# More gate tiles through DRAM, buffers from the room, weight splits on VectorE

## The chip, the cores and the metric

The kernel runs on one core of one Trainium2 chip. The metric is device time in microseconds from start to end of one execution; the median of three runs of the kernel before is 2383.82 us (2383.24 to 2390.1). TensorE is called PE, VectorE DVE, ScalarE ACT, GpSimd POOL and SyncE SP in the profile; PEld is TensorE's weight load.

## The reference, cut to what matters

Two blocks run on 512 tokens of width 1024 in float32. The first is a convolution and attention mixer, the second two attention variants followed by a feed-forward over retrieved experts. Only that last part is touched:

```python
def peer_ffn(x, w_q, sub_keys, expert_u, expert_v):       # 512 tokens, 1024 wide
    q = _rms((xt @ w_q).reshape(T, P_HEADS, P_KEY_DIM))    # 8 heads of 2 x 128
    s1 = einsum('thd,hnd->thn', q[..., :half], sub_keys[:, 0])   # 128 keys each
    s2 = einsum('thd,hnd->thn', q[..., half:], sub_keys[:, 1])
    v1, i1 = top_k(s1, 16); v2, i2 = top_k(s2, 16)
    vals, ci = top_k(all sums v1 + v2, 16)
    e = 128 * i1[ci // 16] + i2[ci % 16]                   # of 16384 experts
    g = softmax(vals)
    a = einsum('cd,ckd->ck', xc, expert_u[e])              # 128 experts a token
    w = g * gelu(a)
    return einsum('ck,ckd->cd', w, expert_v[e])
```

## The kernel before, in words

Matrix products keep nearly float32 precision by splitting each operand into a high half (rounded to float32r) and a low half (the rest): `split_into` copies the high half on ACT and subtracts the low half on DVE or POOL, and `mm3` makes three matmuls of each product. `chunk` loads a weight tile of 128x1024 on SP's queue into `wraw` (three buffers) and splits it into `whi` and `wlo` (two buffers each).

All stages up to about 1010 us (`block1`, `block2`) are not touched. `peer` then has three stages.

The **query stage**: for each of 16 half heads `n`, the queries are projected from `w3[n]` (512 tokens by 128), scored against 128 keys, and the best 16 found by searches on DVE (`top16`); after each second half `pairs` and `decode` combine the two. The projection of `n = 0` uses split weights. For the other fifteen, POOL first adds the halves of the input back into the tile `whole` (line 1382), and the weights are multiplied as they are, in full float32 (line 1397).

The **gate stage** (`gates`) turns the chosen experts and gates of the first 384 tokens into a dense matrix `wd` in DRAM, by one-hot matmuls (lines 1457 to 1470).

The **expert loop** (line 1533) runs over 128 blocks `e` of 128 experts for those 384 tokens. `up_tile(e)` multiplies a block of expert_u with the tokens (24 matmuls of 384 columns) and applies the Gelu. Line 1544 multiplies that tile with its gates, the product is split, and 18 matmuls of 512 columns (lines 84 to 86 under line 1554) add it, times the block of expert_v, to six accumulators `y`.

48 up tiles are made ahead, in the query and gate stages, while TensorE has other work too. 27 of these (`AHEAD`) stay in SBUF in tiles `gt`; 21 (`AWAY`, the last blocks) go to DRAM (`ud`, stored on SP's queue, line 1373) and come back in `gl`, three buffers, near the end of the loop (line 1559). The loop makes the other 80 itself, one in each of the first 80 blocks. So both the loop's weight tiles, for up and down, pass through the same three `wraw` and two `whi` and `wlo`; the up tile's low half is subtracted on POOL, the down tile's on DVE.

The last 128 tokens are not computed densely. `gathered` fetches, for each of the 128 chosen experts of a token, its row of expert_u and then of expert_v by an indirect DMA that POOL issues (line 1493) into one of four buffers `r4`. DVE reduces each row of expert_u with the tokens (line 1498) and adds each row of expert_v, weighted (line 1508). The 256 rows are spread over the loop by `work.advance`, 2.75 to a block in the first 80 blocks. `issue_after(self.pool_last)` keeps a gather behind the last subtract on POOL.

A scheduler sets each engine's order from the program; each engine then runs its own list in order and waits for semaphores.

Of the kernel before, what the change touches and what calls it, by code (L numbers as in the profile page):

```python
# [12 lines left out]
F32 = mybir.dt.float32  # L13
F32R = mybir.dt.float32r
# [4 lines left out]
ALU = mybir.AluOpType  # L19
# [25 lines left out]
class Builder:  # L45
    def __init__(self, tc, ins, out):
        self.tc = tc
        self.nc = tc.nc
        self.i = ins
        self.out = out  # L50


    def split(self, pool, src, tag, shape=None, bufs=None, hi_engine="act", lo_engine="dve"):
# [34 lines left out]
    def chunk(self, src, n=1024, lo_engine="dve"):  # L88

        nc = self.nc  # L90
        raw = self.wp.tile([128, 1024], F32, tag="wraw", name="wraw", bufs=3)
        hi = self.wp.tile([128, 1024], F32R, tag="whi", name="whi", bufs=2)
        lo = self.wp.tile([128, 1024], F32R, tag="wlo", name="wlo", bufs=2)
        nc.sync.dma_start(raw[:, :n], src)
        self.split_into(raw[:, :n], hi[:, :n], lo[:, :n], lo_engine=lo_engine)
        return hi, lo

    def stack_queries(self, src, q, scale=1.0):

# [1146 lines left out]
    def peer(self, hd, xn, xd):  # L1246


        nc, tc, bp = self.nc, self.tc, self.bp
        NT = 384  # L1250
        AHEAD = 27
        AWAY = 21
        NREST = 4
        with ExitStack() as s5:
            wk = s5.enter_context(tc.tile_pool(name="work5", bufs=1))
            ps = self.ps
            ps.share(mm="c", y2="d", y0="b", y1="b", y3="b", y4="a", y5="a")
            T = lambda tag, bufs=1, dt=F32, shape=(128, 512): wk.tile(list(shape), dt, tag=tag, name=tag, bufs=bufs)
# [3 lines left out]
            ud = self.dram.tile([AWAY, 128, NT], F32, name="ud")  # L1262
# [100 lines left out]
            def up_tile(e, lo_engine="pool"):  # L1363
                c = self.chunk(self.i["pu"][e], lo_engine=lo_engine)
                p = P()
                for k in range(8):
                    s = slice(k * 128, (k + 1) * 128)
                    self.mm3(p[:, :NT], (c[0][:, s], c[1][:, s]), (xn[0][k][:, :NT], xn[1][k][:, :NT]), k == 0, k == 7)
                away = e >= 128 - AWAY
                g = T("gs", 2, shape=(128, NT)) if away else T("gt", AHEAD, shape=(128, NT))  # L1370
                nc.scalar.activation(g, p[:, :NT], AF.Gelu_apprx_tanh)
                if away:
                    nc.sync.dma_start(ud[e - 128 + AWAY], g)
                else:
                    up[e] = g

            first_tiles = iter([*range(128 - AWAY, 128), *range(AHEAD)])


            whole = T("big", 2, shape=(128, 8, 512))  # L1380
            for k in range(8):
                nc.gpsimd.tensor_tensor(whole[:, k], xn[0][k], xn[1][k], op=ALU.add)

            for n in range(16):
                hd8, half = n // 2, n % 2
                with self.in_order(self.after if n < 2 else []):
                    if n % 4 == 0:
                        keys = T("r4", 4, shape=(128, 2, 512))[:, 0]
                        nc.sync.dma_start(keys, self.i["keys"][n // 4])
                    acc = P()  # L1390
                    if n == 0:
                        self.project(acc, self.chunk(w3[n], lo_engine="pool"), xn)
                    else:
                        w = self.wp.tile([128, 1024], F32, tag="wraw", name="wraw", bufs=3)
                        nc.sync.dma_start(w, w3[n])
                        for k in range(8):
                            nc.tensor.matmul(acc, w[:, k * 128:(k + 1) * 128], whole[:, k], start=k == 0, stop=k == 7)  # L1397
                q = T("r4", 4, shape=(128, 2, 512))[:, 0]
                nc.scalar.copy(q, acc)
                before, sq = sq, TP()  # L1400
                nc.scalar.activation(sq, acc, AF.Square)
                sp = P(f"y{(0, 1, 3, 4, 5)[n % 5]}")
                ks = slice(n % 4 * 128, n % 4 * 128 + 128)
                for b in range(4):
                    bs = slice(b * 128, b * 128 + 128)
                    nc.tensor.matmul(sp[:, bs], q[:, bs], keys[:, ks], start=True, stop=True)
                for b in range(4):
                    top16(val[:, b, hd8, half], idx[:, b, hd8, half], sp[:, b * 128:(b + 1) * 128], 128)
                if half == 1:
                    nc.gpsimd.tensor_tensor(sq, sq, before, op=ALU.add)  # L1410
                    for b in range(4):
                        nc.tensor.matmul(sv[:, b, hd8], sq[:, b * 128:(b + 1) * 128], self.ones[:, 0:2], start=True, stop=True)
                    pairs(hd8)
                    decode(hd8)
                for _ in range((0, 0, 0, 0, 2, 1)[min(n, 4 + n % 2)]):
                    up_tile(next(first_tiles))
# [20 lines left out]
            def gates():  # L1437


                for b in range(NT // 128):  # L1440
                    pt = P("y2")
                    for n, t in enumerate(chosen(b)):
                        nc.tensor.transpose(pt[:, n * 128:(n + 1) * 128], t, self.ident)
                    bs = slice(b * 128, (b + 1) * 128)
                    for n in (0, 2):
                        nc.scalar.copy(iT[n][:, bs], pt[:, n * 128:(n + 1) * 128])
                    second = wk.tile([128, 128, 8], BF16, tag="oh2", name="second", bufs=4)
                    nc.scalar.copy(second, pt[:, 128:256, None].to_broadcast([128, 128, 8]))
                    for tg in range(4):
                        wt = T("big", 2, shape=(128, 128, 32))  # L1450
                        for t4 in range(8):
                            hot = T("r4", 4, shape=(128, 2, 4, 128))
                            t0 = 128 * b + 32 * tg + 4 * t4
                            if t4 % 2 == 0:
                                short = wk.tile([128, 8, 128], BF16, tag="p", name="short", bufs=6)
                                of = second[:, t0 - 128 * b:t0 - 128 * b + 8]
                                nc.vector.tensor_tensor(short.rearrange("p t (a c) -> p t a c", c=8),
                                                        numbers.rearrange("p (a c) -> p a c", c=8)[:, None].to_broadcast([128, 8, 16, 8]),
                                                        of[:, :, None].to_broadcast([128, 8, 16, 8]), op=ALU.is_equal)
                            nc.scalar.copy(hot[:, 1], short[:, t4 % 2 * 4:t4 % 2 * 4 + 4])  # L1460
                            for t in range(4):
                                i1, g = (iT[n][:, t0 + t:t0 + t + 1] for n in (0, 2))
                                nc.vector.tensor_scalar(hot[:, 0, t], iota, i1, g, op0=ALU.is_equal, op1=ALU.mult)  # L1463
                            wp = P(f"y{(0, 1, 3, 4, 5)[t4 % 5]}")
                            for t in range(4):
                                nc.tensor.matmul(wp[:, t * 128:(t + 1) * 128], hot[:, 0, t], hot[:, 1, t], start=True, stop=True)  # L1466
                            nc.scalar.copy(wt[:, :, 4 * t4:4 * t4 + 4], wp.rearrange("p (t n) -> p n t", t=4))
                            yield 0.8
                        if 4 * b + tg < NT // 32 - 1:
                            nc.sync.dma_start(wd[4 * b + tg], wt)  # L1470
                last[0] = wt
# [4 lines left out]
            def gathered():  # L1476
# [11 lines left out]
                yg[0] = T("idx", shape=(128, 1024))  # L1488

                def fetch(src, n, s):  # L1490
                    t = T("r4", 4, shape=(128, 1024))
                    with tc.issue_after(self.pool_last):
                        nc.gpsimd.indirect_dma_start(t, None, src, bass.IndirectOffsetOnAxis(ap=rows[n][:, s:s + 1], axis=0))  # L1493
                    return t
# [38 lines left out]
            for e in range(128):  # L1533
# [19 lines left out]
                        cs = slice(d * 512, d * 512 + 512)  # L1553
                        self.mm3(y[b][d], (xh[:, bs], xl[:, bs]), (c[0][:, cs], c[1][:, cs]), e == 0, e == 127)
                if e + AHEAD < both:
                    up_tile(e + AHEAD)
                if e + 2 >= both and e + 2 < 128:
                    up[e + 2] = T("gl", 3, shape=(128, NT))
                    nc.sync.dma_start(up[e + 2], ud[e + 2 - both])
                steps = both - AHEAD  # L1560
                work.advance((e + 1) / steps * 0.86 if e < steps else 0.86 + (e + 1 - steps) / 36 * 0.15)
            for b in range(4):
                h = T("r4", 4, shape=(128, 1024))
                nc.sync.dma_start(h, hd[b])
                for d in range(2):
                    cs = slice(d * 512, d * 512 + 512)
                    nc.vector.tensor_tensor(h[:, cs], h[:, cs], y[b][d] if b < 3 else yg[0][:, cs], op=ALU.add)
                    nc.sync.dma_start(self.out[b * 128:(b + 1) * 128, cs], h[:, cs])
# [99 lines left out]
```

## Time and profile before

| | us |
|---|---|
| median of 3 runs | 2383.82 |
| the profiled execution | 2386.1 |
| its span | 2384.1 |
| TensorE busy in it | 2261.5 (95%) |
| VectorE busy | 1682.8 (71%) |
| ScalarE busy | 1003.6 (42%) |
| GpSimd busy | 1001.5 (42%) |

The profile shows one execution; its span is the stretch from the first to the last instruction, 2.0 us less than the execution's time. A wait is put down to what released it last. Matmuls overlap, so TensorE's busy time includes slack: its pace is read from start to start. The granted clock was 0.987 of full over the span, and full from 1500 to 2100 us.

### The profile page before, as it was taken

Reading aid. Unit: us, or ns where it says so; the run is one execution under the profiler, and the core shown is the slowest. Engines: PE = TensorE matmul, PEld = TensorE weight load, DVE = VectorE, ACT = ScalarE, POOL = GpSimd, SP = SyncE. Lnnn points to the kernel's source line nnn. Section 1 sums busy time; section 2 is a strip of 40 time slices with the busy share of each in tenths; the row PEclk is TensorE's granted clock in tenths of the full one; section 3 lists DMA queues with packets and bytes.
Section 4 is the critical chain, followed back from the end, with each engine's and each line's share of the span. In section 5 each row is a group of like instructions: output and inputs, shape, how many; then the busy total and the mean of one; then the engine's idle time right before and its main releaser. Section 6 shows DMA issues by size and latency. Waiting matters only on the chain.

```text
span 2384.1 us, 31933 instructions
## 1 busy us (share of the span) xinstructions
PE 2261.5 (95%) x11207; PEld 1906.0 (80%) x11207; DVE 1682.8 (71%) x3504; ACT 1003.6 (42%) x1766; POOL 1001.5 (42%) x829
## 2 busy tenths in 40 slices
PE   6999999999998889899999998999999999999999
PEld 4888888888886668767789998888888878877787
DVE  7766666533457887676789966777767877778875
ACT  4544444422344688622238762333333333323332
POOL 4221121000034657455520006767777767776410
PEclk9999999999999999899999999999999999999999
DMA  3222222333342122333345558988888988889984
GB/s 116 80 82 87 80 80 88 125 94 94 96 126 75 54 71 98 120 97 118 116 135 199 208 196 292 313 297 284 286 290 296 305 281 281 296 281 325 348 306 154
DMA packets 166833, 433.26 MB, mean 182 GB/s; under 512 B 14608, under 2 KB 69392, under 8 KB 165136
## 3 DMA queue, kind: packets, MB, share of 16 engines
q1 hardware_dynamic: 129808, 296.98, 38.5%
q0 software_dynamic: 36864, 134.23, 16.0%
q8 instruction: 88, 1.44, 0.3%
q14 instruction: 73, 0.60, 0.1%
HBM read 391.91 MB, written 38.21 MB: 180 GB/s over the span
## 4 chain that ended last, share of the span: by engine, by line
PE 70%; DVE 10%; DMA 9%; issue 5%; POOL 4%; ACT 2%; DVEq 0%; SPq 0%; POOLq 0%; ACTq 0%
PE mm L86 11%; PE mm L84 10%; PE mm L85 10%; DMA r<-pun_in,row 6%; PE y L85 4%; PE y L86 4%; PE y L1466 4%; PE mm L1397 3%; PE y L84 3%; POOL wlo L71 3%; PE g L86 2%; PE g L85 2%; PE g L84 2%; PE s L367 2%; DMA r<-pv_in,row 2%
## 5 line engine op out<-in xcount | busy, mean ns | idle before, releaser
L65 ACT CAST whi<-wraw 128x1024 fp32r<-128x1024 f32 (+2 forms) x398 | 414.1, 1041 | 742.3 <-PE y L86 281.3
L71 POOL TENSOR_TENSOR wlo<-wraw,whi 128x1024 fp32r<-128x1024 f32 (+3 forms) x124 | 311.6, 2514 | 649.7 <-ACT whi L65 648.5
L86 PE MATMUL mm<-uh,wlo 128*128 128x384 f32 (+1 forms) x1512 | 543.7, 360 | 6.8 <-POOL wlo L71 5.0
L84 PE MATMUL mm<-uh,whi 128*128 128x384 f32 (+1 forms) x1512 | 545.5, 361 | 4.4 <-ACT whi L65 4.1
L85 PE MATMUL mm<-ul,whi 128*128 128x384 f32 (+1 forms) x1512 | 539.9, 357 | 3.6 <-DVE ul L71 3.6
L71 DVE TENSOR_TENSOR wlo<-wraw,whi 128x1024 fp32r<-128x1024 f32 (+1 forms) x274 | 341.6, 1247 | 180.3 <-ACT whi L65 180.1
L85 PE MATMUL y<-wlo,p 128*128 128x512 f32 x768 | 306.9, 400 | 48.2 <-DVE wlo L71 48.0
L86 PEld LDWEIGHTS mm<-uh,wlo 128*128 128x128 f32 x1512 | 285.6, 189 | 36.4 <-POOL wlo L71 17.0
L84 PEld LDWEIGHTS mm<-uh,whi 128*128 128x128 f32 x1512 | 286.1, 189 | 29.8 <-ACT whi L65 4.5
L85 PEld LDWEIGHTS mm<-ul,whi 128*128 128x128 f32 x1512 | 286.0, 189 | 28.3 <-DVE ul L71 3.8
L1498 DVE CUSTOM_DVE_ANT_0 r<-r,val 128x1024 f32<-128x1024 f32 x128 | 226.2, 1783 | 110.0 <-DMA r<-pun_in,row 109.1
L86 PE MATMUL y<-whi,p 128*128 128x512 f32 x768 | 301.3, 393 | 0.0
L1508 DVE SCALAR_TENSOR_TENSOR idx<-r,act,idx 128x1024 f32<-128x1024 f32 x127 | 211.0, 1661 | 76.4 <-DMA r<-pv_in,row 74.9
L1493 POOL DMA_INDIRECT r<-pv_in,row x128 | 189.7, 1482 | 81.4 <-DVE idx L1508 44.7
L85 PEld LDWEIGHTS y<-wlo,p 128*128 128x128 f32 x768 | 144.8, 189 | 97.8 <-DVE wlo L71 67.4
L1493 POOL DMA_INDIRECT r<-pun_in,row x128 | 187.5, 1465 | 42.2 <-issue 20.6
L84 PE MATMUL y<-whi,p 128*128 128x512 f32 x768 | 197.6, 392 | 0.0
L65 ACT CAST p<-p 128x384 fp32r<-128x384 f32 x128 | 65.8, 514 | 292.3 <-DVE p L1544 290.7
L86 PEld LDWEIGHTS y<-whi,p 128*128 128x128 f32 x768 | 144.9, 189 | 30.0
L84 PEld LDWEIGHTS y<-whi,p 128*128 128x128 f32 x768 | 143.0, 188 | 25.3 <-ACT whi L65 0.5
L372 ACT ACTIVATE p<-p,st 128x128 f32<-128x128 f32 (+3 forms) x160 | 89.6, 561 | 71.5 <-DVE st L371 70.6
L1463 DVE TENSOR_SCALAR r<-iota,iT,iT 128x128 f32<-128x128 f32 x384 | 104.6, 342 | 19.9 <-PE y L1466 19.9
(605 smaller groups left out, 3763.0 us busy)
## 6 DMA issues: line engine op xcount, KB each, us to landing
wraw<-w_in SPq DMA_DIRECT2D x145, 512.0 KB, 3.5
wraw<-pu_in SPq DMA_DIRECT2D x128, 512.0 KB, 5.5
wraw<-pv_in SPq DMA_DIRECT2D x128, 512.0 KB, 5.0
wd<-big SPq DMA_DIRECT2D x12, 2048.0 KB, 7.3
big<-wd SPq DMA_DIRECT2D x31, 768.0 KB, 6.1
hd<-h SPq DMA_DIRECT2D x24, 256.0 KB, 2.2
h<-hd SPq DMA_DIRECT2D x16, 256.0 KB, 3.7
ud<-gs SPq DMA_DIRECT2D x21, 192.0 KB, 2.0
```

The source lines that it names most:

```text
L65: nc.scalar.copy(hi, src)
L71: i = eng.tensor_tensor(lo, src, hi, op=ALU.subtract)
L84: mm(out, w[0], x[0], start=start, stop=False)
L85: mm(out, w[0], x[1], start=False, stop=False)
L86: mm(out, w[1], x[0], start=False, stop=stop)
L372: nc.scalar.activation(pi, pi, AF.Exp, bias=st[:, 0:1], scale=-1.0, accum_out=st[:, 1:2])
L1397: nc.tensor.matmul(acc, w[:, k * 128:(k + 1) * 128], whole[:, k], start=k == 0, stop=k == 7)
L1463: nc.vector.tensor_scalar(hot[:, 0, t], iota, i1, g, op0=ALU.is_equal, op1=ALU.mult)
L1466: nc.tensor.matmul(wp[:, t * 128:(t + 1) * 128], hot[:, 0, t], hot[:, 1, t], start=True, stop=True)
L1493: nc.gpsimd.indirect_dma_start(t, None, src, bass.IndirectOffsetOnAxis(ap=rows[n][:, s:s + 1], axis=0))
L1498: nc.vector.tensor_tensor_reduce(t, t, xn3, 1.0, 0.0, ALU.mult, ALU.add, act[:, s:s + 1])
L1508: nc.vector.scalar_tensor_tensor(yg[0], t, act[:, s:s + 1], yg[0], op0=ALU.mult, op1=ALU.add)
```

## The change

Of the 48 tiles made ahead, 11 stay in SBUF and 37 go to DRAM, stored from ScalarE's queue. The room of 16 tiles goes to two more raw weight tiles, one more pair of split tiles (of a second pool, used in turn by `weight_tile`) and two more row buffers. The loop's up tiles are split on VectorE (`up_tile(e + AHEAD, "dve")`); those of the query stage stay on GpSimd. All sixteen query projections use split weights, the first two with GpSimd's subtract, the others with VectorE's; `whole` is gone.

```diff
     def chunk(self, src, n=1024, lo_engine="dve"):
-        raw = self.wp.tile([128, 1024], F32, tag="wraw", name="wraw", bufs=3)
-        hi = self.wp.tile([128, 1024], F32R, tag="whi", name="whi", bufs=2)
-        lo = self.wp.tile([128, 1024], F32R, tag="wlo", name="wlo", bufs=2)
+        raw = self.weight_tile(F32, "wraw", 3, 2)
+        hi = self.weight_tile(F32R, "whi", 2, 1)
+        lo = self.weight_tile(F32R, "wlo", 2, 1)
...
+    def weight_tile(self, dt, tag, bufs, more):
+        pool = self.wp
+        if self.more is not None:
+            n = self.turns[tag] = self.turns.get(tag, -1) + 1
+            if n % (bufs + more) >= bufs:
+                pool, tag, bufs = self.more, tag + "2", more
+        return pool.tile([128, 1024], dt, tag=tag, name=tag, bufs=bufs)
...
-        AHEAD = 27
-        AWAY = 21
+        AHEAD = 11
+        AWAY = 37
...
+            self.more = wk
...
-                    nc.sync.dma_start(ud[e - 128 + AWAY], g)
+                    nc.scalar.dma_start(ud[e - 128 + AWAY], g)
...
-            whole = T("big", 2, shape=(128, 8, 512))
-            for k in range(8):
-                nc.gpsimd.tensor_tensor(whole[:, k], xn[0][k], xn[1][k], op=ALU.add)
...
-                    if n == 0:
-                        self.project(acc, self.chunk(w3[n], lo_engine="pool"), xn)
-                    else:
-                        w = self.wp.tile([128, 1024], F32, tag="wraw", name="wraw", bufs=3)
-                        nc.sync.dma_start(w, w3[n])
-                        for k in range(8):
-                            nc.tensor.matmul(acc, w[:, k * 128:(k + 1) * 128], whole[:, k], start=k == 0, stop=k == 7)
-                q = T("r4", 4, shape=(128, 2, 512))[:, 0]
+                    self.project(acc, self.chunk(w3[n], lo_engine="pool" if n < 2 else "dve"), xn)
+                q = T("r4", 6, shape=(128, 2, 512))[:, 0]
...
-                    t = T("r4", 4, shape=(128, 1024))
+                    t = T("r4", 6, shape=(128, 1024))
...
-                    up_tile(e + AHEAD)
+                    up_tile(e + AHEAD, "dve")
```

The other tiles of tag `r4` get six buffers likewise.

How the engines' orders move, in the first 80 blocks of the expert loop. VectorE before, a block and the beginning of the next (L1498 is a gathered row, `wlo` a low half of weights, `p` the product and its low half):

```order
L71 TENSOR_TENSOR wlo<-wraw,whi 128x1024
L1498 ISA r_14236,act<-r_14236,val 128x1024
L1498 ISA act 128x1
L1498 ISA r_14239,act<-r_14239,val 128x1024
L1498 ISA act 128x1
L1498 ISA r_14242,act<-r_14242,val 128x1024
L1498 ISA act 128x1
L71 TENSOR_TENSOR p<-p 128x384
L1544 TENSOR_TENSOR p<-gt,big 128x384
L71 TENSOR_TENSOR wlo<-wraw,whi 128x1024
```

And VectorE now, a like stretch:

```order
L72 TENSOR_TENSOR wlo_15086<-wraw,whi_15085 128x1024
L1498 ISA r_15192,act<-r_15192,val 128x1024
L1498 ISA act 128x1
L72 TENSOR_TENSOR wlo<-wraw,whi 128x1024
L1498 ISA r_15195,act<-r_15195,val 128x1024
L1498 ISA act 128x1
L72 TENSOR_TENSOR p<-p 128x384
L1544 TENSOR_TENSOR p<-gt,big 128x384
L72 TENSOR_TENSOR wlo<-wraw_15156,whi 128x1024
```

Two low halves now stand between the rows of each block where one stood.

GpSimd before, in the same loop (L1493 issues a gather):

```order
L1493 DMA r_14451<-pun_in,row_13505 128x1024
L1493 DMA r_14454<-pun_in,row_13505 128x1024
L1493 DMA r_14457<-pun_in,row_13505 128x1024
L71 TENSOR_TENSOR wlo<-wraw,whi 128x1024
L1493 DMA r_14523<-pun_in,row_13505 128x1024
```

And GpSimd now:

```order
L1493 DMA r_14618<-pun_in,row_13812 128x1024
L1493 DMA r_14621<-pun_in,row_13812 128x1024
L1493 DMA r_14689<-pun_in,row_13812 128x1024
L1493 DMA r_14692<-pun_in,row_13812 128x1024
L1493 DMA r_14758<-pun_in,row_13812 128x1024
```

No subtract is left between the gathers of the loop.

TensorE before, the down matmuls of one block (L84 high half by high half, L85 low half of the weights, L86 low half of the product):

```order
L84 MATMUL y0_13430<-whi_19368,p_19375 128x512
L84 MATMUL y1_13431<-whi_19368,p_19375 128x512
L84 MATMUL y2_13432<-whi_19368,p_19375 128x512
L84 MATMUL y3_13433<-whi_19368,p_19375 128x512
L84 MATMUL y4_13434<-whi_19368,p_19375 128x512
L84 MATMUL y5_13435<-whi_19368,p_19375 128x512
L85 MATMUL y0_13430<-wlo_19369,p_19375 128x512
L86 MATMUL y0_13430<-whi_19368,p_19376 128x512
```

And now (the three lines are 85 to 87):

```order
L85 MATMUL y0_13737<-whi_18934,p_18941 128x512
L86 MATMUL y0_13737<-wlo_18935,p_18941 128x512
L87 MATMUL y0_13737<-whi_18934,p_18942 128x512
L85 MATMUL y1_13738<-whi_18934,p_18941 128x512
L86 MATMUL y1_13738<-wlo_18935,p_18941 128x512
L87 MATMUL y1_13738<-whi_18934,p_18942 128x512
```

The low half of the weights is asked for by the second matmul of a block where it was the seventh.

## Rows read from the trace of the kernel before

**Rows 1.** Windows of four stages: us; PE, PEld, DVE, ACT, POOL; clock, DMA, GB/s.
```profile
1020.00:1235.00 215.00, 212.88 (x940) 155.72 (x939) 159.38 (x856) 52.81 (x77) 101.92 (x115) 0.99 0.38 119
1235.00:1425.00 190.00, 190.00 (x1364) 189.81 (x1364) 165.08 (x474) 138.49 (x251) 3.13 (x2) 1.00 0.55 197
...
1500.00:2100.00 600.00, 557.15 (x2733) 487.77 (x2732) 457.13 (x489) 192.24 (x262) 435.61 (x245) 1.00 0.87 292
...
2165.00:2240.00 75.00, 70.82 (x307) 56.55 (x306) 64.60 (x72) 26.44 (x35) 41.80 (x27) 1.00 0.94 332
```

**Rows 2.** Windows, instructions of line 1544 alone: us, DVE busy, clock, DMA, GB/s.
```profile
1490.00:2150.00 660.00, 39.56 (x72) 1.00 0.87 292
```

**Rows 3.** Timeline of PE in the loop: start, us, engine, line, what.
```profile
1510.32 0.40 PE L86 MATMUL y<-whi,p 128*128 128x512 f32 x1
...
1512.62 0.39 PE L86 MATMUL y<-whi,p 128*128 128x512 f32 x1
...
1512.85 0.34 PE L84 MATMUL mm<-uh,whi 128*128 128x384 f32 x1
...
1517.04 1.54 PE L84 MATMUL y<-whi,p 128*128 128x512 f32 x6
```

**Rows 4.** Waits from 1500 to 2100 us: total, times, longest.
```profile
ACT whi L65 <- PE y L86: 164.6, 64, 3.0
POOL wlo L71 <- ACT whi L65: 102.2, 35, 5.1
DVE r L1498 <- DMA r<-pun_in,row: 91.1, 56, 4.0
...
DVE idx L1508 <- DMA r<-pv_in,row: 49.3, 29, 3.5
PE y L85 <- DVE wlo L71: 39.1, 31, 2.3
```

**Rows 5.** Groups by shape, 1500 to 2100 us: count, busy, mean ns, idle before.
```profile
L1498 DVE CUSTOM_DVE_ANT_0 r<-r,val 128x1024 f32<-128x1024 f32 x112 | 198.9, 1794 | 91.9 <-DMA r<-pun_in,row 91.1
...
L71 POOL TENSOR_TENSOR wlo<-wraw,whi 128x1024 fp32r<-128x1024 f32 x65 | 174.2, 2680 | 103.2 <-ACT whi L65 102.2
...
L1508 DVE SCALAR_TENSOR_TENSOR idx<-r,act,idx 128x1024 f32<-128x1024 f32 x67 | 123.5, 1844 | 50.5 <-DMA r<-pv_in,row 49.3
...
L71 DVE TENSOR_TENSOR wlo<-wraw,whi 128x1024 fp32r<-128x1024 f32 x66 | 80.2, 1216 | 0.0
...
L1544 DVE TENSOR_TENSOR p<-gt,big 128x384 f32<-128x384 f32 x65 | 35.7, 549 | 0.0
```

**Rows 6.** Lines 1498 and 1508, whole loop: ns min/median/max, first and last start.
```profile
L1498 DVE CUSTOM_DVE_ANT_0 r<-r,val x128: 1209/1226/3623, 1441.9 to 1870.0; 128x1024 f32<-128x1024 f32 x128
...
L1508 DVE SCALAR_TENSOR_TENSOR idx<-r,act,idx x127: 1271/1285/3466, 1874.9 to 2286.3; 128x1024 f32<-128x1024 f32 x127
```

**Rows 7.** Timeline, VectorE's rows beside GpSimd.
```profile
1501.18 2.50 POOL L71 TENSOR_TENSOR wlo<-wraw,whi 128x1024 fp32r<-128x1024 f32 x1
...
1502.50 2.27 DVE L1498 CUSTOM_DVE_ANT_0 r<-r,val 128x1024 f32<-128x1024 f32 x1 [1.07 <-DMA r<-pun_in,row]
...
1503.84 1.76 POOL L1493 DMA_INDIRECT r<-pun_in,row  x1 [0.15 <-issue]
...
1504.93 1.23 DVE L1498 CUSTOM_DVE_ANT_0 r<-r,val 128x1024 f32<-128x1024 f32 x1 [0.16 <-DMA r<-pun_in,row]
```

**Rows 8.** DMA queues, 1500 to 2100 us: packets, MB, share of 16 engines.
```profile
q0 software_dynamic: 25795, 93.94, 44.9%
q1 hardware_dynamic: 43552, 80.75, 41.8%
```

**Rows 9.** Timeline of GpSimd and TensorE as the query stage begins.
```profile
1011.52 10.10 POOL L1382 TENSOR_TENSOR big<-uh,ul 128x512 f32<-128x512 f32 x8
...
1016.62 13.90 PE L1397 MATMUL mm<-big,wraw 128*128 128x512 f32 x32
```

**Rows 10.** Line 1373: ns min/median/max of its issues.
```profile
L1373 SPq DMA_DIRECT2D ud<-gs x21: 319/326/424, 1055.8 to 1233.4; - x21
```

More of the change, by code (lines that the diff above doesn't have):

```diff
@@ L50, in __init__ @@
         self.out = out
+        self.more, self.turns = None, {}
     def split(self, pool, src, tag, shape=None, bufs=None, hi_engine="act", lo_engine="dve"):
@@ L1387, in peer @@
                     if n % 4 == 0:
-                        keys = T("r4", 4, shape=(128, 2, 512))[:, 0]
+                        keys = T("r4", 6, shape=(128, 2, 512))[:, 0]
                         nc.sync.dma_start(keys, self.i["keys"][n // 4])
                     acc = P()
-                    if n == 0:
-                        self.project(acc, self.chunk(w3[n], lo_engine="pool"), xn)
-                    else:
-                        w = self.wp.tile([128, 1024], F32, tag="wraw", name="wraw", bufs=3)
-                        nc.sync.dma_start(w, w3[n])
-                        for k in range(8):
-                            nc.tensor.matmul(acc, w[:, k * 128:(k + 1) * 128], whole[:, k], start=k == 0, stop=k == 7)
-                q = T("r4", 4, shape=(128, 2, 512))[:, 0]
+                    self.project(acc, self.chunk(w3[n], lo_engine="pool" if n < 2 else "dve"), xn)
+                q = T("r4", 6, shape=(128, 2, 512))[:, 0]
                 nc.scalar.copy(q, acc)
@@ L1451, in gates @@
                         for t4 in range(8):
-                            hot = T("r4", 4, shape=(128, 2, 4, 128))
+                            hot = T("r4", 6, shape=(128, 2, 4, 128))
                             t0 = 128 * b + 32 * tg + 4 * t4
@@ L1562, in peer @@
             for b in range(4):
-                h = T("r4", 4, shape=(128, 1024))
+                h = T("r4", 6, shape=(128, 1024))
                 nc.sync.dma_start(h, hd[b])
```

## The prediction, made before the change was run

> **What bounds the kernel now.** I first read busy time by stage [rows 1]; each row gives the stretch, then PE, PEld, DVE, ACT and POOL busy with their instruction counts, the granted clock, the DMA share and GB/s. The query stage (1020 to 1235 us) and the gate stage (1235 to 1425) have TensorE at 212.9 of 215 and 190 of 190 us: there only less matmul work helps. The expert loop is different: from 1500 to 2100 us TensorE is 557 of 600 busy, VectorE 457, GpSimd 436, and the DMA engines 87%. No one of them is full, so I looked for the pace each would allow.
>
> The multiply of line 1544 runs once an expert: 72 from 1490 to 2150 us [rows 2], 9.17 us each. TensorE's own pace is read from start to start, since its matmuls overlap [rows 3]: the 24 of an up tile take 1517.04 - 1512.85 = 4.19 us, and ten steps among the down matmuls 1512.62 - 1510.32 = 2.30 us, so 18 take 4.14. Together 8.33 us. The loop loses 0.84 us an expert to waiting, 60 us over 72 experts, and the 93% hides it.
>
> The waits name the loss [rows 4]. TensorE waits 39 us for VectorE's low half of the down weights (short waits that the overlap of matmuls hides come on top). VectorE waits 91 + 49 = 140 us for gathered rows, 2.16 us for each of the 65 experts in that stretch. ScalarE waits 165 us for the down matmuls to release a high-half buffer, and GpSimd 102 us for ScalarE's copy. They form a ring: with two split buffers the copy is late; GpSimd's subtract waits for it with the gathers queued behind; so rows are late, and on VectorE the next down subtract stands behind a late row.
>
> **The change, part by part, against the profiled execution's 2386.1 us (2.3 above the median of 2383.8).**
>
> *The up subtract moves to VectorE; GpSimd keeps the gathers.* In 65 experts VectorE ran 66 subtracts of 1.216 us, 65 times two instructions of 0.55 us (the product of line 1544 and the low half of that product, of the same size), and 112 + 67 gathered rows of mean 1.794 and 1.844 us [rows 5]; it was busy 457 / 65 = 7.03 us an expert. The same rows have medians of 1.226 and 1.285 us [rows 6], so some are stretched. Two rows side by side show where [rows 7]: the one started at 1502.50, inside GpSimd's subtract (1501.18 to 1503.68), took 2.27 us; the one at 1504.93, inside a gather's issue alone (1503.84 to 1505.60), took 1.23. The stretching comes to 112 x 0.568 + 67 x 0.559 = 101 us, 1.56 an expert. If it goes with the subtract, VectorE pays 1.22 and gets 1.56 back: 2 x 1.216 + 2 x 0.55 + 112/65 x 1.226 + 67/65 x 1.285 = 6.97 us, against 7.03 now. If the gather's issue were to blame, it would be 7.03 + 1.22 = 8.25. I take 6.97, for the row beside an issue alone was short; 8.25 is the other end.
>
> The Trainium skill, page "SBUF — State Buffer", section "Who interferes with whom", says that a VectorE instruction with two SBUF inputs and a GpSimd instruction that reads SBUF shut each other out for a whole instruction, and that descriptor generation should not contend with `tensor_tensor`. By that rule all stretching goes and the sum is the one with 6.97; were the rows read the other way, VectorE alone would ask for 8.25. The 2.27 us row agrees with the rule.
>
> GpSimd falls from a subtract of 2.680 us [rows 5], its wait and the gathers to the gathers alone: 179/65 issues of at most 1.76 us [rows 7], under 4.9 us an expert: a gather can start as soon as a row buffer is free. ScalarE keeps its work (192 / 65 = 2.96 us an expert), and nothing is queued behind it that gets later.
>
> *Five raw tiles, three split tiles, six rows.* The third split tile lets ScalarE copy one tile, about 4.1 us, earlier; that takes the ring apart at the release wait (165 us) and covers VectorE being late. It must, for the down matmuls now ask for the low half second instead of seventh, 0.23 instead of 1.4 us after the high half. Six rows at 8.5 / 2.75 = 3.1 us each give a gather 18 us from issue to use, against 12.
>
> *What is late next is the DMA.* Its queues were busy 44.9 + 41.8 = 86.7% [rows 8] of 9.23 us, 8.0 us an expert; that work is unchanged, for the loop loads the same bytes. At TensorE's 8.33 us the engines would be 96% busy. The fullest long stretch with both queues is 94% (2165 to 2240, [rows 1]), so I take 8.0 / 0.94 = 8.5 us an expert: 72 x (9.17 - 8.5) = **48 us saved**. The ends are 8.33 (60 us) and 9.17 (nothing).
>
> *The queries' weights are split.* Fifteen projections lose their eight full-f32 matmuls: 32 records took 13.90 us [rows 9], so 16 (one projection) take 6.95. They get 24 matmuls of 0.23, 5.52 us. TensorE is full in this stage: 15 x 1.43 = 21 us less. Added are 15 copies on ScalarE (53 of 215 us busy there, so hidden) and 14 subtracts on VectorE, 17 us beside 159 of 215: hidden on average, but they stand in order among the top-16 searches, each of which waits for a projection. GpSimd's sum of the two halves (10.10 us, [rows 9]) goes as well; it lay beside the first projections. I take **18 us saved**; the ends are 0, if VectorE's order holds TensorE up, and 31, the 21 plus the whole sum.
>
> *Sixteen more tiles through DRAM, stored from ScalarE.* A store held SP 0.326 us [rows 10]; 37 on ScalarE are about 12 us, spread over 405 us in which it is half idle (191 of 405 busy, [rows 1]): nothing. SP no longer waits for a Gelu before the next weight load, also nothing, since loads were not what ended waits there. The stores go into stages with the DMA at 38 and 55%. The 16 extra loads fall into the last 48 experts: 192 KB at the 332 GB/s of 2165 to 2240 is 0.6 us of DMA each, 10 us in all, where the engines are already 94% busy. Against that, those 48 experts took 2384 - 2165 = 219 us where 48 x 4.14 = 199 and the final stores would do, and the spare buffers reach some of it. I take **0**, ends +10 and -12.
>
> Sum: -48 - 18 + 0 = -66, so 2320 us against the profiled execution, **2318 us** against the median.
>
> **Rivals.**
> 1. *VectorE still waits for rows.* Its two subtracts and the rows stand in one order. If the rows keep their 2.16 us of waiting, 6.97 + 2.16 = 9.13 us an expert: the loop gains 3 us and only the query stage pays, about 2363 (2345 to 2372). For it: with the DMA fuller, a row lands later. Against: the waits of [rows 4] come from gathers issued late, and six buffers with a free GpSimd issue them earlier.
> 2. *TensorE's pace is reached.* If the transfers are packed better than 94%, 8.33 us and the 21 us of the query stage give -81, about 2303, and with the last experts and the sum of the halves down to 2280.
> 3. *VectorE becomes the bound, and the kernel slower.* If the gather's issue stretches the rows and the waits stay, an expert costs 8.25 + 2.16 = 10.4 us: 72 x 1.24 = +89, less 18, 2455. It decides from 9.17 + 18/72 = 9.42 us an expert on. Against it stands the 1.23 us row of [rows 7]. The Trainium skill, page "Perfetto Trace Analysis", section "Optimizing Scalar/DVE Operations", advises to move work off a saturated VectorE, even to GpSimd, which is this rival's side; it adds that a port shared by the two may make that useless. VectorE at 76% is not saturated, so I give the advice little weight.
> 4. *No change*: the query stage loses what it gains, the loop stays at 9.13: about 2381.
>
> **How the numbers follow.** Forecast (2300 to 2345) 0.60, rival 1 0.17, rival 2 0.11, rival 3 0.08, rival 4 0.04. Faster by over 0.3% (7 us, about what a measurement of this kernel tells from none) is 0.60 + 0.17 + 0.11 = 0.88, within it 0.04, slower 0.08. The range 2280 to 2370 leaves out rivals 3 and 4 and the far ends of 1 and 2, some 0.17.
>
> **What would show it.** Right: VectorE's gathered rows all near 1.23 and 1.29 us; TensorE's waits for the low half nearly gone; 8.4 to 8.6 us an expert with the DMA above 92%; the loop beginning 15 to 20 us earlier. Wrong in the loop: VectorE's waits for rows still near 2 us an expert (rival 1), or long rows beside gather issues (rival 3). Wrong in the query stage: TensorE waiting for VectorE's low half there. If the last 48 experts take over 229 us, the DRAM loads cost more than I gave them.

## The result and the profile after

| | before | changed |
|---|---|---|
| median, us | 2383.53 (4 runs beside it) | 2277.15 (2276.43 to 2278.35, 4 runs) |
| ratio, 95% interval | 1 | 0.9552 (0.953 to 0.9573) |
| span of the profiled execution | 2384.1 | 2275.8 |

The changed kernel is 106 us faster. The forecast was 2318 us with a range of 2280 to 2370: the sign was right, the time lies 3 us outside the range, on the fast side. The starts of the loop's 128 multiplies (line 1544) cut the two spans into the parts of the forecast (us):

| part | before | after | difference | forecast |
|---|---|---|---|---|
| up to the first multiply of the loop | 1425.7 | 1401.7 | -24 | -18 |
| experts 1 to 8 | 64.4 | 54.6 | -10 | not counted |
| experts 9 to 80 | 663.9 (9.22 each) | 596.9 (8.29 each) | -67 | -48 |
| the other 48, to the end | 230.0 | 222.6 | -7 | 0 |

The windows of the changed kernel, with the columns of [rows 1] (us; PE, PEld, DVE, ACT, POOL; clock, DMA share, GB/s), for the query stage, the gate stage, the loop, and the last experts:

```profile
1020.00:1215.00 195.00, 194.95 (x1081) 180.90 (x1080) 173.35 (x901) 67.19 (x94) 102.85 (x114) 1.00 0.43 133
1215.00:1400.00 185.00, 185.00 (x1344) 184.85 (x1343) 157.74 (x461) 135.36 (x248) 6.20 (x4) 1.00 0.61 219
1500.00:2000.00 500.00, 500.00 (x2538) 455.86 (x2537) 417.75 (x518) 177.66 (x243) 235.82 (x180) 1.00 0.95 340
...
2160.00:2260.00 100.00, 100.00 (x438) 81.84 (x437) 54.76 (x75) 36.26 (x50) 0.00 (x0) 1.00 0.62 191
```

TensorE is now busy 500 of 500 us in the loop, where it was 557 of 600, and the DMA share is 95% at 340 GB/s, above the 94% that the forecast took for a ceiling. From 1020 to 2260 us TensorE is idle for 4 us in all, nearly all of it as the loop begins.

The multiplies alone, as [rows 2]:

```profile
1490.00:2050.00 560.00, 37.41 (x68) 1.00 0.95 341
```

560 / 68 is 8.24 us each where it was 9.17. TensorE's own pace by [rows 3] is 8.33, a reading of a few matmuls, so nothing is lost to waiting any more.

The waits from 1500 to 2000 us (total, times, longest), as [rows 4]:

```profile
ACT whi L66 <- issue: 170.5, 59, 2.9
ACT whi L66 <- PE mm L86: 140.6, 61, 2.5
POOL r L1493 <- DVE act L1498: 135.9, 73, 4.8
POOL r L1493 <- DVE idx L1508: 114.9, 61, 4.9
DVE wlo L72 <- ACT whi L66: 47.6, 78, 1.6
```

In no row does TensorE wait, nor VectorE for a gathered row: the 91 + 49 us of [rows 4] have turned round. GpSimd now waits 251 us for VectorE to free a row buffer, that is, it issues gathers as early as it can. Its wait for ScalarE's copy (102 us) is gone with the subtract.

The groups by shape of the same stretch (count, busy, mean ns, idle before), as [rows 5], and lines 1498 and 1508 over the whole loop (ns min/median/max, first and last start), as [rows 6]:

```profile
L72 DVE TENSOR_TENSOR wlo<-wraw,whi 128x1024 fp32r<-128x1024 f32 x122 | 149.2, 1223 | 47.7 <-ACT whi L66 47.6
...
L1498 DVE CUSTOM_DVE_ANT_0 r<-r,val 128x1024 f32<-128x1024 f32 x95 | 114.2, 1219 | 0.0
L1508 DVE SCALAR_TENSOR_TENSOR idx<-r,act,idx 128x1024 f32<-128x1024 f32 x84 | 107.7, 1282 | 0.8
```

```profile
L1498 DVE CUSTOM_DVE_ANT_0 r<-r,val x128: 1214/1218/1225, 1400.6 to 1760.4; 128x1024 f32<-128x1024 f32 x128
...
L1508 DVE SCALAR_TENSOR_TENSOR idx<-r,act,idx x127: 1273/1279/1323, 1765.5 to 2119.5; 128x1024 f32<-128x1024 f32 x127
```

The longest of 255 rows takes 1.32 us, where it was 3.62. The rows also end at 2119 and not 2286 us. The scheduler now gives VectorE 3 rows an expert (2.97 in experts 9 to 80) instead of 2.75, for no subtract on GpSimd holds the gathers to their block; in e1 below, with that subtract back, it is 2.74 again.

The DMA queues from 1500 to 2000 us (packets, MB, share of 16 engines), as [rows 8]:

```profile
q0 software_dynamic: 25872, 94.18, 50.8%
q1 hardware_dynamic: 40716, 75.28, 43.6%
```

### The profile page after: what moved, and what is told of

It reads as the page before. It is cut to its first block, busy times and chain, and to the rows that moved or that the text cites. A ratio compares the mean times of both kernels' runs of the same rounds, so it can differ in the third digit from the quotient of the medians.

```text
span 2275.8 us, 32121 instructions
## 1 busy us (share of the span) xinstructions
PE 2214.0 (97%) x11327; PEld 1931.3 (85%) x11327; DVE 1658.8 (73%) x3598; ACT 1013.3 (45%) x1781; POOL 744.1 (33%) x742
## 4 chain that ended last, share of the span: by engine, by line
PE 88%; DVE 6%; ACT 2%; issue 2%; DMA 1%; POOL 1%; SPq 0%; POOLq 0%; DVEq 0%; ACTq 0%
PE mm L87 13%; PE mm L85 13%; PE mm L86 13%; PE y L85 8%; PE y L86 8%; PE y L87 8%; PE y L1466 4%; PE g L87 3%; PE g L86 3%; PE g L85 3%; PE s L377 2%; PE pt L403 2%; PE o L407 1%; PE o L406 1%; DVE wlo L72 1%
## 5 line engine op out<-in xcount | busy, mean ns | idle before, releaser
L72 DVE TENSOR_TENSOR wlo<-wraw,whi 128x1024 fp32r<-128x1024 f32 x368 | 457.9, 1245 | 259.7 <-ACT whi L66 259.5
L87 PE MATMUL mm<-uh,wlo 128*128 128x384 f32 (+1 forms) x1632 | 585.9, 359 | 4.5 <-DVE wlo L72 4.5
L86 PE MATMUL mm<-ul,whi 128*128 128x384 f32 (+1 forms) x1632 | 586.1, 359 | 3.5 <-DVE ul L72 3.5
L85 PE MATMUL mm<-uh,whi 128*128 128x384 f32 (+1 forms) x1632 | 587.3, 360 | 0.3 <-DVE ul L154 0.3
L86 PEld LDWEIGHTS mm<-ul,whi 128*128 128x128 f32 x1632 | 308.4, 189 | 29.9 <-DVE ul L72 3.8
L85 PEld LDWEIGHTS mm<-uh,whi 128*128 128x128 f32 x1632 | 308.2, 189 | 27.1 <-DVE ul L154 0.7
L85 PE MATMUL y<-whi,p 128*128 128x512 f32 x768 | 300.7, 392 | 0.0
L86 PE MATMUL y<-wlo,p 128*128 128x512 f32 x768 | 300.4, 392 | 0.0
L87 PE MATMUL y<-whi,p 128*128 128x512 f32 x768 | 291.5, 390 | 0.0
L1493 POOL DMA_INDIRECT r<-pun_in,row x128 | 167.4, 1308 | 362.2 <-PE y L1466 174.9
L1493 POOL DMA_INDIRECT r<-pv_in,row x128 | 171.1, 1337 | 185.2 <-DVE idx L1508 163.4
L72 POOL TENSOR_TENSOR wlo<-wraw,whi 128x1024 fp32r<-128x1024 f32 (+3 forms) x45 | 101.1, 2251 | 311.2 <-ACT whi L66 311.1
L85 PEld LDWEIGHTS y<-whi,p 128*128 128x128 f32 x768 | 144.2, 188 | 28.8 <-ACT p L66 0.3
L86 PEld LDWEIGHTS y<-wlo,p 128*128 128x128 f32 x768 | 144.3, 188 | 27.4
L1508 DVE SCALAR_TENSOR_TENSOR idx<-r,act,idx 128x1024 f32<-128x1024 f32 x127 | 162.8, 1282 | 1.1
L1498 DVE CUSTOM_DVE_ANT_0 r<-r,val 128x1024 f32<-128x1024 f32 x128 | 153.7, 1219 | 13.4 <-PE y L1466 7.5
L72 DVE TENSOR_TENSOR p<-p 128x384 fp32r<-128x384 f32 x128 | 71.3, 557 | 93.3 <-PE y L86 91.4
```

The costliest lines, as they stand in the source:

```text
L72: i = eng.tensor_tensor(lo, src, hi, op=ALU.subtract)
L85: mm(out, w[0], x[0], start=start, stop=False)
L86: mm(out, w[0], x[1], start=False, stop=False)
L87: mm(out, w[1], x[0], start=False, stop=stop)
L1498: nc.vector.tensor_tensor_reduce(t, t, xn3, 1.0, 0.0, ALU.mult, ALU.add, act[:, s:s + 1])
L1508: nc.vector.scalar_tensor_tensor(yg[0], t, act[:, s:s + 1], yg[0], op0=ALU.mult, op1=ALU.add)
```

## The experiments

Fifteen more kernels ran. "Start" is the first multiply of the loop, "an expert" the mean of experts 9 to 80, "rest" the time from the 81st to the end of the span, all in the profiled execution.

| run | median us | ratio to before (95%) | start | an expert | rest |
|---|---|---|---|---|---|
| before | 2383.53 | 1 | 1425.7 | 9.22 | 230.0 |
| changed | 2277.15 | 0.9552 (0.953, 0.9573) | 1401.7 | 8.29 | 222.6 |
| e1_pool_sub | 2303.45 | 0.9685 (0.9664, 0.9706) | 1397.0 | 8.48 | 234.8 |
| e2_two_split | 2292.66 | 0.9636 (0.9615, 0.9656) | 1412.6 | 8.32 | 222.9 |
| e12_two_split_pool | 2366.36 | 0.9947 (0.9928, 0.9966) | 1406.6 | 9.14 | 242.9 |
| e7_dve_alone | 2305.34 | 0.969 (0.9671, 0.9708) | 1422.7 | 8.29 | 224.5 |
| e14_no_room | 2290.49 | 0.9607 (0.9566, 0.9648) | 1407.8 | 8.29 | 223.5 |
| e3_four_rows | 2276.09 | 0.9567 (0.9547, 0.9587) | 1399.0 | 8.26 | 223.4 |
| e4_three_raw | 2341.19 | 0.9839 (0.9818, 0.986) | 1401.8 | 9.18 | 222.9 |
| e11_three_raw_held | 2278.52 | 0.9574 (0.9557, 0.9592) | 1398.2 | 8.23 | 232.9 |
| e13_held | 2276.51 | 0.9548 (0.9507, 0.9588) | 1398.5 | 8.28 | 227.0 |
| e9_more_dma | 2320.97 | 0.9732 (0.9691, 0.9773) | 1416.1 | 8.22 | 259.1 |
| e15_pool_writes | 2351.92 | 0.9863 (0.9843, 0.9883) | 1459.7 | 8.37 | 228.0 |
| e16_pool_reads | 2407.29 | 1.0092 (1.0058, 1.0126) | 1423.8 | 9.64 | 226.9 |
| e17_pool_clears | 2367.36 | 0.9919 (0.989, 0.9949) | 1424.3 | 9.18 | 228.5 |
| e5_whole | 2299.77 | 0.967 (0.9652, 0.9688) | 1423.9 | 8.29 | 222.4 |
| e6_sp_store | 2280.38 | 0.9561 (0.952, 0.9601) | 1405.1 | 8.29 | 222.2 |

### Which part made the loop faster

*The changed kernel with the up subtract on GpSimd again:*

```diff
-                    up_tile(e + AHEAD, "dve")
+                    up_tile(e + AHEAD)
```

> The changed kernel, with the loop's up subtract back on GpSimd; buffers, stores and queries as changed. Theory A (the third split pair took the ring apart, whoever subtracts): 8.3 to 8.5 us a block, the loop's first 80 blocks at most 15 us longer than in the changed kernel (2277 to 2292). Rival B (it is the subtract that left GpSimd): the gathered rows are stretched again to a mean near 1.8 us and come late, 8.9 us a block or more, 2320 or more.

*The changed kernel with two split pairs:*

```diff
-        hi = self.weight_tile(F32R, "whi", 2, 1)
-        lo = self.weight_tile(F32R, "wlo", 2, 1)
+        hi = self.weight_tile(F32R, "whi", 2, 0)
+        lo = self.weight_tile(F32R, "wlo", 2, 0)
```

> The changed kernel with two split pairs instead of three, VectorE still subtracting. Theory A: ScalarE's copy waits again for the down matmuls, and TensorE asks for the low half second: 8.9 us a block or more, 2320 or more. Rival B: VectorE is on time without the lock and the late rows, at most 8.5 us a block, 2277 to 2292.

*Both edits together:*

> The changed kernel with both taken back: two split pairs and the loop's up subtract on GpSimd; five raw tiles, six rows, queries and stores as changed. If the ring needs both the late subtract and two split buffers (each alone having cost 15 and 26 us): 9.0 to 9.2 us a block, 2335 to 2355. If the longer lead of loads and rows is what freed the loop: at most 8.6 us a block, 2300 to 2315.

*The kernel before with the subtract alone moved.* Since no subtract on GpSimd then paces the rows, VectorE's rows are held behind the up subtract of their block, so that their order is 2.75 a block as before:

```diff
+        elif self.hold:
+            self.dve_last = i.ins
...
+                    with tc.issue_after(self.dve_last):
                         nc.vector.tensor_tensor_reduce(t, t, xn3, ...)
...
-                    up_tile(e + AHEAD)
+                    self.hold = True
+                    up_tile(e + AHEAD, "dve")
+                    self.hold = False
```

> The kernel before with one change: the loop's up subtract on VectorE, rows held in the program's order; two split pairs, three raw tiles, four rows, 27 tiles kept, queries as before. Theory B (the subtract's place is enough): 8.3 to 8.6 us a block, 2320 to 2340. Theory A (the ring of two split buffers stays): 9.0 us a block or more, 2365 to 2385.

*That, with the queries' weights split as in the changed kernel, and no tile or buffer more:*

> The kernel before with the two changes of place alone: the loop's up subtract on VectorE (rows held in the program's order) and the queries' weights split; 27 tiles kept, 21 stored by SP, three raw tiles, two split pairs, four rows. If the DRAM tiles and the room they make give only what two split pairs cost in the changed kernel (15 us): 2285 to 2297. If they give nothing: 2275 to 2283. If they matter together: 2300 or more.

Time of an expert in the four cases:

| | subtract on GpSimd | subtract on VectorE |
|---|---|---|
| two split pairs | 9.14 (e12) | 8.32 (e2), 8.29 (e7) |
| three split pairs | 8.48 (e1) | 8.29 (changed) |

With GpSimd's subtract and two pairs, e12 has six rows, five raw tiles and 37 tiles in DRAM, and its loop is where it was before. Either cure takes most of the 0.9 us, so the two gains don't add. Moving the subtract gives all of it, with rows held (e7) or not (e2). The times of e1 and e12 lie 11 us above the ranges expected of their loops, most of it behind the 80th expert (234.8 and 242.9 us). The rows from 1500 to 2000 us show the ring whole in e12 and open in e7. First the waits of e12, then one of its groups:

```profile
POOL wlo L72 <- ACT whi L66: 100.0, 33, 6.1
DVE r L1498 <- DMA r<-pun_in,row: 85.4, 49, 3.8
...
DVE idx L1508 <- DMA r<-pv_in,row: 32.7, 21, 3.1
...
PE y L86 <- DVE wlo L72: 29.4, 21, 2.6
```

```profile
L1498 DVE CUSTOM_DVE_ANT_0 r<-r,val 128x1024 f32<-128x1024 f32 x103 | 181.5, 1784 | 85.6 <-DMA r<-pun_in,row 85.4
```

Then e7 (its line 1502 is line 1498), the same group and the window of that stretch:

```profile
L1502 DVE CUSTOM_DVE_ANT_0 r<-r,val 128x1024 f32<-128x1024 f32 x106 | 124.6, 1219 | 1.1 <-DMA r<-pun_in,row 1.1
```

```profile
1500.00:2000.00 500.00, 500.00 (x2531) 455.43 (x2530) 393.83 (x514) 180.94 (x242) 252.60 (x166) 1.00 0.94 324
```

e7 has the same two split pairs, and fewer row buffers and raw tiles (four and three); its waits for rows of expert_u are 1 us where e12 has 85, and TensorE is full. The third pair still earns 15 us beside VectorE's subtract (2292.66 against 2277.15), 11 of them ahead of the loop. In the query stage of e2 TensorE is not full, where the changed kernel has 194.95 of 195:

```profile
1020.00:1215.00 195.00, 189.56 (x1034) 173.47 (x1033) 178.46 (x884) 61.23 (x88) 104.50 (x112) 0.99 0.40 125
```

e14 without any of the room (2290.49) and e2 with all of it but the third pair (2292.66) can't be told apart: their intervals overlap. So the 16 tiles in DRAM pay for that pair, and for nothing else that a run here shows.

### Rows and raw tiles

*Four row buffers instead of six* (each `T("r4", 6, ...)` to 4), *three raw tiles instead of five* (`self.weight_tile(F32, "wraw", 3, 0)`), *three raw tiles with the rows held as in e7, and the changed kernel with the rows held:*

> The changed kernel with four row buffers instead of six. Theories A and B: VectorE waits somewhat longer for rows, but the third split pair covers it, 0 to +12 us (2277 to 2289). Rival C (the six rows keep VectorE from waiting, and that is what freed TensorE): a wait for rows of 1 us a block or more and 8.7 us a block, 2310 or more.

> The changed kernel with three raw weight tiles instead of five. Theories A and B: 0 to +8 us, since ScalarE's copy did not wait for loads before. Rival D (with the DMA engines 95% busy only the longer lead of five loads keeps TensorE fed): TensorE waits for weight loads again, 8.6 us a block, 2300 or more.

> Three raw tiles again, but VectorE's gathered rows are held in the program's order, behind the up subtract of their block (2.75 rows a block by the order, where the run with three raw tiles alone had 4). Theory E (that run was slow because its rows ran ahead and filled the DMA engines early, not for want of raw tiles): 8.3 to 8.4 us a block and 2277 to 2290. Rival D (the lead of five loads is needed at this DMA share): 8.8 us a block or more, 2315 to 2345.

> The changed kernel with the rows held in the program's order (2.75 a block instead of 3.0), the base for the run with more DMA. TensorE's pace either way: 8.28 us a block; the rows left over fall into the blocks after the first 80. Same time within 6 us (2273 to 2283); if the earlier rows were what kept the end short, 2284 or more.

Six rows are worth nothing in the changed kernel. Three raw tiles seemed to cost 64 us, but e4 did more than its edit: the scheduler, with other buffers, gave VectorE 4 rows a block. Its windows while rows ran, and after:

```profile
1440.00:1900.00 460.00, 423.04 (x2042) 375.97 (x2041) 393.70 (x507) 144.71 (x197) 279.38 (x196) 0.96 0.97 355
1900.00:2100.00 200.00, 192.04 (x956) 172.40 (x955) 138.71 (x143) 66.54 (x92) 57.84 (x42) 0.99 0.79 276
```

In the first of them, of its waits:

```profile
ACT whi L66 <- DMA wraw<-pu_in: 47.4, 15, 7.4
```

ScalarE now waits for weight tiles still on their way, which it doesn't in the changed kernel: four rows an expert ask for more than the DMA gives in 8.3 us. The DMA moves 355 GB/s at 97%, and TensorE is short of 37 us in 460. TensorE's granted clock averages 0.96 there, with 34 of the 460 us at 1.2 GHz instead of 2.4, where it is 1.00 in the same stretch of the changed kernel. With the rows held at 2.75 (e11), three raw tiles cost nothing; four rows with five raw tiles were not run. Holding them with five (e13) changes nothing either, so the 3 rows an expert of the changed kernel don't explain its gain.

### Is the DMA the bound?

*e13, with every load of gates in the loop (`wd` into `w`, 768 KB for four experts) issued twice; the second copy serves nothing:*

```diff
+                    load = nc.sync.dma_start(w[:, :n], wd[:n, :, e:e + 4, :].rearrange("g p e t -> p g e t"))
                     load = nc.sync.dma_start(w[:, :n], wd[:n, :, e:e + 4, :].rearrange("g p e t -> p g e t"))
```

> The changed kernel with rows held in the program's order and the gate tile of every four blocks loaded twice into the same place: 1536 more packets of 512 bytes, which at 27 ns on 16 engines is 0.65 us of DMA a block on top of some 7.6 to 7.8. If the DMA engines bind just above the changed loop's demand: 8.45 to 8.7 us a block with a DMA share of 97% or more, 2292 to 2312. If they had room left: at most 8.35 us a block, 2277 to 2285.

The same window in e13 and in e9:

```profile
1480.00:1980.00 500.00, 500.00 (x2536) 455.56 (x2535) 403.39 (x509) 175.29 (x243) 243.53 (x168) 1.00 0.94 326
...
1480.00:1980.00 500.00, 500.00 (x2540) 456.15 (x2539) 391.64 (x508) 176.04 (x243) 204.36 (x159) 1.00 0.98 345
```

At 98% TensorE is still full, 8.22 us an expert. The 44 us that e9 costs lie outside. The loop starts 17.6 us later than in e13: its first multiply waits for the second copy of the first gates, issued at 1399.9 us and landed at 1416.0. The last 48 experts, which take TensorE 4.1 us each and want gates twice as often, are 32 us longer. Here too the kernel did more than its edit: the scheduler left 188 rows in experts 9 to 80 where e13 has 197, and 50 in the last 48 where e13 has 41. So e9 moves 6% more in the window and not all that its gates add, and its last 48 experts hold more rows as well. In experts 9 to 80 the DMA does not bind TensorE at 95%, nor at e9's 98%; by e4 it does where a fourth row is asked for with three raw tiles.

### What a subtract on GpSimd costs

Three kernels keep VectorE's low half (e7) and give GpSimd work back that serves nothing; 23 up tiles stay in SBUF instead of 27, to make room for a spare tile. *e15: after ScalarE's copy of the up weights, three clearings of a spare tile, and a copy of eight of its numbers on ScalarE. e16: one subtract of the high half from itself:*

```diff
+            junk = self.junk_pool.tile([128, 1024], F32, tag="junk", name="junk", bufs=1)
+            self.pool_last = nc.gpsimd.tensor_tensor(junk, hi, hi, op=ALU.subtract).ins
```

*e17: the clearings of e15, tied to the copy:*

```diff
+            nc.scalar.copy(self.junk[:, 0:8], hi[:, 0:8])
+            for _ in range(3):
+                i = nc.gpsimd.memset(self.junk[:, 0:1024], 0.0)
+            self.pool_last = i.ins
```

> The kernel before with the loop's up subtract on VectorE (2305.34 us, 8.31 us an expert), and added to it, in each expert of the loop, GpSimd work that serves nothing: after ScalarE's copy of the up weights GpSimd clears a spare tile three times, reading nothing, and the gathers stand behind it as they stood behind the subtract; four spare tiles fewer stay in SBUF. VectorE still makes the low half. If the loss came from gathers that queue behind GpSimd's wait and work, the waits for rows return: 9.0 us an expert or more, 2355 to 2385 us. If it came from GpSimd and VectorE shutting each other out when both read SBUF, the rows stay at 1.23 and 1.29 us and the time is 2303 to 2315. If it was the lateness of the low half itself, the same 2303 to 2315, and the next kernel shows the same.

> As the run above, but what GpSimd does after ScalarE's copy is one subtract of a tile of 128x1024 from itself, into a spare tile that nobody uses: a wait, a queue and a subtract as in the kernel before, with two SBUF inputs, while the low half still comes from VectorE. Shutting out: rows stretched to 1.8 us in the mean, 9 us an expert or more, 2355 to 2385 us. Queueing: the same time as the run above, both high. Lateness of the low half alone: 2303 to 2315 in both.

> The run with GpSimd's three clearings once more, for there the scheduler had moved them out of the loop into the query and gate stages, where nothing held them back. Now each block's ScalarE copies eight numbers of the high half into the spare tile first, so that the clearings (0.96 us each, 2.9 us together, nothing read from SBUF by GpSimd) wait for ScalarE's copy of the up weights, with the gathers behind them. The low half comes from VectorE. If queueing behind that wait was the loss: rows wait again, 9.0 us an expert or more, 2355 to 2410 us, like the run with the unused subtract (2407.29). If GpSimd's reading of SBUF beside VectorE was the loss: rows at 1.23 and 1.29 us, 8.3 to 8.5 us an expert, 2303 to 2330 us.

e15 told nothing. Line 102, its clearings (ns min/median/max, first and last start), lies wholly ahead of its loop, which starts at 1459.7:

```profile
L102 POOL MEMSET junk<- x240: 941/956/1112, 1021.1 to 1450.1; 128x1024 f32 x120
```

The scheduler had put them where nothing held them, and ScalarE's copies of eight numbers waited for them there; 37 of its 47 us over e7 are the late start. e16, groups from 1500 to 2000 us, with the waits behind, and last its rows over the whole loop as in [rows 6] (1506 is line 1498):

```profile
L1506 DVE CUSTOM_DVE_ANT_0 r<-r,val 128x1024 f32<-128x1024 f32 x111 | 167.5, 1518 | 76.7 <-DMA r<-pun_in,row 76.6
...
L101 POOL TENSOR_TENSOR junk<-whi 128x1024 f32<-128x1024 f32 x52 | 123.9, 2383 | 119.3 <-ACT whi L66 118.9 <-issue 0.2
```

```profile
POOL junk L101 <- ACT whi L66: 118.9, 46, 6.6
DVE r L1506 <- DMA r<-pun_in,row: 76.6, 59, 4.0
```

```profile
L1506 DVE CUSTOM_DVE_ANT_0 r<-r,val x128: 1210/1224/2918, 1442.0 to 1883.4; 128x1024 f32<-128x1024 f32 x128
```

e17, groups and waits (1509 is line 1498, 1520 line 1508):

```profile
L102 POOL MEMSET junk<- 128x1024 f32 x165 | 157.7, 956 | 104.9 <-ACT junk L100 97.8 <-ACT gt L1381 0.5
...
L1509 DVE CUSTOM_DVE_ANT_0 r<-r,val 128x1024 f32<-128x1024 f32 x108 | 131.8, 1223 | 89.9 <-DMA r<-pun_in,row 87.3 <-issue 2.2
```

```profile
POOL junk L102 <- ACT junk L100: 97.8, 48, 4.3
DVE r L1509 <- DMA r<-pun_in,row: 87.3, 50, 3.4
...
DVE idx L1520 <- DMA r<-pv_in,row: 31.2, 18, 3.1
...
PE y L88 <- DVE wlo L72: 27.4, 20, 2.4
```

e17 decides between stretched rows and queueing. In its loop no low half comes from GpSimd and no row is stretched (mean 1.223 us), yet an expert takes 9.18 us, and the waits are those of e12 and of [rows 4]: 98 us of GpSimd for ScalarE's copy, 87 + 31 us of VectorE for rows, then TensorE for VectorE. What cost the time was the queue: gathers standing behind an instruction of GpSimd that waits for ScalarE. How much of it is the wait and how much the 2.9 us of clearing itself no run separates. e16, with GpSimd reading SBUF and the rows stretched again, takes 0.46 us an expert more than e17, with one subtract more on VectorE than before; how much of that is the stretching no run shows.

### The query stage and the stores

*The changed kernel with `whole` and fifteen full-float32 projections as before, and with the stores on SP's queue:*

```diff
-                    nc.scalar.dma_start(ud[e - 128 + AWAY], g)
+                    nc.sync.dma_start(ud[e - 128 + AWAY], g)
```

> The changed kernel with the queries' weights not split, as before (the sum of the halves on GpSimd and full-f32 matmuls for fifteen projections). By the predicted term, 18 us more, 2295; by TensorE's matmul work and the sum alone, 21 to 31 us more, 2298 to 2308. Rival: the earlier start of the loop came from the buffers and the stores instead, and this costs under 8 us.

> The changed kernel with the 37 stores on SP's queue instead of ScalarE's. By the predicted term nothing: 2274 to 2281. Rival: a store that waits for its Gelu holds the weight loads behind it on SP's queue, and the query and gate stages get 5 us or more longer (2282 or more).

The split is worth 22 us, all of it ahead of the loop (start 1423.9 against 1401.7). The stores from ScalarE start the loop 3.4 us earlier than those from SP; in the ratios that difference is within the intervals.

## Why the prediction was wrong, step by step

- **The ring: right.** TensorE's 8.33 us, the 0.84 us lost, and the chain from a late copy over gathers queued on GpSimd to a late low half on VectorE: e17 rebuilds it with GpSimd's clearings, two pairs and VectorE's subtract, and takes 9.18 us an expert where before takes 9.22.
- **VectorE's order: right.** The rows came down to 1.22 and 1.28 us, no wait for rows took the place of the old one (rival 1), and gather issues stretch nothing (rival 3). The rule of the Trainium skill cited there ("SBUF — State Buffer", "Who interferes with whom") agrees with all of it: rows reach 1.5 us in the mean beside GpSimd's subtract (e16), and stay at 1.22 beside clearings (e17). But the 1.56 us an expert of stretching was not what the loss needed: e17 has the loss without it. The sum of 6.97 us adds durations, while the 7.03 beside it counts overlapping ones once; the durations of [rows 5] add up to 7.33, so the relief was larger than the text says.
- **The third split tile: half right.** The text gave it the release wait and the loop. In the loop it replaces most of the moved subtract (e1, 8.48) or adds nothing to it (e2, 0.03 us); it earns its 15 us mainly in the query stage, of which the text did not speak.
- **The failed step: "What is late next is the DMA."** The forecast divided 8.0 us of DMA work by the fullest stretch seen, 94%, and took 8.5 us an expert. Both numbers fell. The 94% was no ceiling: the loop runs at TensorE's pace, 8.29 us an expert, at 95% and, in e9, at 98%; the stretch at 94% had only been the fullest that the old kernel asked for. Nor was the work fixed: 94.4% of 8.29 us is 7.8 us an expert, with more rows in it. Before, 86.7% of 600 us moved 174.7 MB [rows 8], 2.98 us a MB; now 94.4% of 500 us moves 169.5 MB, 2.79. In e13, with the rows of before, it is 2.88; why a MB takes less is not shown. Rival 2, TensorE's pace, was the case that came, with a chance of 0.11. Of the 42 us by which the parts of the span miss the forecast, 19 are this step.
- **A term left out.** The 48 us were counted over 72 experts of the window from 1490 us, and nothing was said of the first eight, which gave 10 us. It is not the loss of the loop: e12 and e17, which keep that loss, take 55.5 and 54.6 us there, where before takes 64.4 and the changed kernel 54.6. What gave the 10 us stays open.
- **The query stage: mis-sized.** 24 us where 18 were taken. The matmuls' 21 us were about right (e5: 22, GpSimd's sum of the halves with it); the discount for VectorE's order was not needed with three split pairs. With two something of it is: e2 starts 13 us earlier than before, and e14 15 us earlier than e7.
- **The last 48 experts: mis-sized.** -7 where 0 was taken, within the ends given. (The text's 219 us count from 2165; from the multiply of the 81st it is 230.) In the trace of before, TensorE waits 4.4 us for VectorE's low half after its last up tile; in the changed kernel it does not wait there. The window above shows no work of GpSimd and a DMA share of 62% from 2160 to 2260 us, where rows still ran before. e7, with the moved subtract and none of the room, has 224.5 us, so most of the 7 us comes with the subtract; other kernels with VectorE's subtract and held rows, e13 and e11, have 227 and 233, and why is open.
- **Stores from ScalarE, six rows, five raw tiles: nothing, as forecast**, to within the 3 us of e6.

No kernel here beats the changed one: e3, with four rows, and e13, with the rows held, are the same to 1 us, and TensorE is all but full from the query stage on.

## What to carry to other kernels

Ask of each engine what stands in its queue behind an instruction that waits: a 2.7 us subtract on a GpSimd with time to spare (436 of 600 us busy) cost 0.9 us an expert, with two split pairs, through the gathers behind it, and three clearings of a spare tile there cost as much. A DMA share of 94% that a stalled kernel shows is what that kernel asked for and no ceiling; test it by adding transfers. When a loss is a ring, one cut link may give it all back, so price the cuts together and not one by one.

## What was not expected of the hardware

- The DMA engines held TensorE's loop at a share of 98% and 345 GB/s (e9), and reached 355 GB/s over 460 us where more was asked (e4).
- A VectorE row of 128x1024 takes 1.22 us beside GpSimd's clearings of a tile of that size (e17) and beside its gather issues (the changed kernel), but up to 2.92 us in e16, beside a subtract with two inputs in SBUF.
